# Hybrid block on one Trainium2 core: the two experts picked early run once with 128 places

## Chip, cores and metric

The kernel runs on one core of a Trainium2 chip. The metric is device time in microseconds (us), the median of the timed runs. Three runs of the kernel before took 1964.92, 1969.21 and 1973.45 us.

## What is computed

One layer: a mixer (short convolution and gated DeltaNet), its output projection with a residual, then a mixture of experts with a residual, then a final norm. The change lies in the mixture of experts:

```python
gate, expert_id = ...          # for each of 2048 tokens: one of 4 groups, then the best 2 of its 8 experts
def expert_block(args):        # blocks of tokens of one expert, D = 1024, FF = 512
    xblk, e = args
    return (silu(xblk @ w_gate[e]) * (xblk @ w_up[e])) @ w_down[e]
out = jnp.zeros((N + 1, D)).at[slot_tok].add(yb * slot_gate[:, None])
return rms_norm(x + out, final_norm_g)
```

## The kernel before, in words

All matrices are split into a high and a low float16 half, so each product is three matmuls. The kernel runs in three stages: the mixers; the output projection with the router; the experts.

**Output projection and router.** A loop over 16 tiles of 128 tokens. `tile_a` (L970 to L994) multiplies by `w_out`, adds the residual and writes the normed tile to `h2_d` in DRAM. `tile_b` (L1003 to L1014) turns the tile (8 transposes per half) and makes the 36 router logits. After every 4 tiles (a block of 512 tokens) `route(b)` (L837 to L921) finds, on VectorE, group, experts and each token's place in its expert, and adds them to a table in PSUM (`tabT`, L887).

**The picked experts.** After two blocks `pick` chooses the three experts with the fewest tokens so far (`NSP = 3`), so that their weights are loaded while the projection still runs. Two of them (`NST = 2`) are called job 0 and job 1 here; the third is job 2. Jobs 0 and 1 run in two passes: `first` takes 96 places filled by the first three blocks, fetched in the loop's tile 14; `second` takes 48 places of the last block. `route(2)` and `route(3)` each read the table and write the places (`tabE`, L894; `entries`, L949 to L953), and after `route(2)` a correction (L915 to L920) moves the last block's tokens behind place 96. While `route(3)` and `ranks` (L1193 to L1214, which sorts the other experts by their number of tokens and writes their numbers, `eid`) run on VectorE, TensorE runs the `first` passes: `weave` traces both in turns.

**An expert's work.** `fetch` or `gather` reads the tokens' rows by an indirect DMA of GpSimd (`xr`, L1028) and their gates (L1033); `turn` transposes them (L1044) and copies them to `xT` (L1045); `gate_up` is 192 matmuls (L1059); `down` is 24 matmuls of 512 columns (L1094) if the expert has one chunk of at most 128 places, else 96 matmuls with the operands the other way round (L1129) and transposes back (L1116); ScalarE scales the result by the gate (`yo`, L1103, L1120); GpSimd adds it to `acc_d` in DRAM (L1072).

**Weights.** Each expert has 20 loads on SyncE's queue (L766 twice for each of 8 pieces of gate and up, L775 four times for down): 16 of 256 KB and 4 of 512 KB. They land in staging buffers `mst` (10 of 512 KB at this stage); ScalarE and VectorE (`split`, L92 and L93) make the halves in `wgu` and `wd`, of which there are two each. So job j+2's halves can be made only when `gate_up` of job j is through. The number of the expert is read on SyncE by `value_load` (L1429) from `sid` (the picked ones) or from `eid`.

**Order.** The 32 jobs follow one another; the two outermost of the ranked ones alternate (few and many places), the last three also carry the final norm. A scheduler then places the instructions on the queues by priority; each engine runs its queue in order.

The lines that set it up (before):

```python
C1, C2 = 96, 48
CAPS = [C1 + C2, C1 + C2, 136, 216, 188, 176, 172, 164, ...]
weave((prio(seq(tile_b(NT - 1), route(NB - 1), fetch(second[0]), fetch(second[1]), ranks()),200), 20, 0, 1),
      (seq(gate_up(first[0]), down(first[0]), added(first[0]), gate_up(first[1]), down(first[1]), added(first[1])), 2 * (GU + 6), 0, 1),
      (turn(first[1]), 2, 0.2, 0.4), (prio(turn(second[0]), PT), 2, 0.8, 0.95))
```

## Time and profile before

| | us |
|---|---|
| median of 3 timed runs | 1969.21 |
| span of the profiled execution | 1978.5 |
| TensorE busy | 1774.9 (90%) |
| VectorE busy | 1407.2 (71%) |
| ScalarE busy | 1017.3 (51%) |
| GpSimd busy | 476.2 (24%) |

For the profiled execution only its span, from its first to its last instruction, is given; it is 9.3 us longer than the median of the timed runs. Times in the views are us from the start of that span. The mixers end near 890 us, the projection's last matmul of the loop is at 1146 us, the experts' last matmul at 1907 us, and the rest is the final norm. A busy share is an average over all of these; the change touches the stretch from 1110 us to 1250 us, so that stretch is read by itself.

### The profile page before, as it was taken

The numbers are of one execution on the slowest core, as the hardware profiler recorded it, in microseconds if no ns is written. First come the engines' busy times: TensorE is split into PE (matmuls) and PEld (weight loads), VectorE is DVE, ScalarE is ACT, GpSimd is POOL, SyncE is SP. The second block draws the span as 40 slices with busy tenths as digits, with TensorE's granted clock in tenths as the row PEclk, the third lists the DMA queues.
The fourth block names the chain that finished last, engine by engine and source line by source line (L and its number), as shares of the span: only waits on it lengthen the run. The fifth ranks groups of instructions, "written<-read, shape, count | busy, mean of one in ns | idle before, by whom it ended". The sixth has DMA issues, their size and how long they took to land. (4 is left out here: it accounts for less than half of the span.)

```text
span 1978.5 us, 43091 instructions
## 1 busy us (share of the span) xinstructions
PE 1774.9 (90%) x16783; PEld 1218.3 (62%) x16783; DVE 1407.2 (71%) x2756; ACT 1017.3 (51%) x1700; POOL 476.2 (24%) x408
## 2 busy tenths in 40 slices
PE   6789999999999999999999988998889999999820
PEld 5455555555555554444454466888888999999720
DVE  8889888888888745323246748887778888888623
ACT  6654435345344323211334546776667777767522
POOL 1321211121121100000000114333222443443366
PEclk9889999999999999999999998999999999999965
DMA  4222002002001023002357858999999999999853
GB/s 141 66 67 52 10 15 51 10 16 52 9 13 45 25 66 114 27 17 59 130 173 254 294 169 269 336 312 304 290 308 362 347 334 356 341 342 299 281 162 138
DMA packets 203763, 329.25 MB, mean 166 GB/s; under 512 B 45021, under 2 KB 99366, under 8 KB 203554
## 3 DMA queue, kind: packets, MB, share of 16 engines
q1 hardware_dynamic: 177010, 264.90, 39.9%
q0 software_dynamic: 22016, 52.48, 10.3%
q10 hardware_dynamic: 4528, 9.06, 1.2%
q8 instruction: 133, 2.18, 0.5%
q14 instruction: 76, 0.62, 0.1%
HBM read 276.21 MB, written 54.53 MB: 167 GB/s over the span
## 5 line engine op out<-in xcount | busy, mean ns | idle before, releaser
L134 PE MATMUL acc<-hT,whl 128*128 128x512 f16 x2640 | 635.0, 381 | 0.2 <-DVE hT L203 0.2
L1059 PE MATMUL a<-xT,wgu 128*128 128x136 f16 (+19 forms) x6528 | 407.7, 225 | 22.8 <-DVE sl L1066 13.7
L1059 PEld LDWEIGHTS <-wgu 128*128 128x128 f16 x6528 | 399.3, 100 | 30.4 <-issue 25.9
L134 PEld LDWEIGHTS <-whl 128*128 128x128 f16 x2640 | 253.0, 99 | 248.2 <-issue 11.2
L93 DVE SCALAR_TENSOR_TENSOR wgu<-mst,gw,wgu 128x1024 f16<-128x1024 f32 x256 | 317.2, 1277 | 15.8 <-ACT wgu L92 15.8
L92 ACT ACTIVATE wgu<-mst,gw 128x1024 f16<-128x1024 f32 x256 | 279.0, 1138 | 31.3 <-DMA mst<-in_w_up_dram 28.2
L979 PE MATMUL a<-wo,yb 128*128 128x512 f16 x768 | 178.0, 384 | 0.0
L1072 POOL DMA_INDIRECT acc_d<-yo,tabS x53 | 106.0, 1999 | 257.1 <-ACT yo L1120 200.3
L93 DVE SCALAR_TENSOR_TENSOR wd<-mst,wd 128x1024 f16<-128x1024 f32 x128 | 154.5, 1215 | 6.2 <-ACT wd L92 6.2
L1129 PE MATMUL a<-ac,wd 128*128 128x136 f16 (+12 forms) x1920 | 142.8, 230 | 2.7 <-issue 1.2
L92 ACT ACTIVATE wd<-mst 128x1024 f16<-128x1024 f32 x128 | 130.7, 1045 | 19.4 <-DMA mst<-in_w_down_dram 17.3
L1129 PEld LDWEIGHTS <-wd 128*128 128x128 f16 x1920 | 130.2, 98 | 5.7 <-issue 3.9
L979 PEld LDWEIGHTS <-yb 128*128 128x128 f16 x768 | 72.5, 99 | 80.5 <-issue 5.4
L294 DVE SCALAR_TENSOR_TENSOR cv<-raw,pcol,cv 128x512 f32<-128x512 f32 x144 | 114.9, 800 | 1.6
L1028 POOL DMA_INDIRECT xr<-h_d,tabG x54 | 69.5, 1286 | 171.7 <-PE t L1044 161.8
L1066 DVE SCALAR_TENSOR_TENSOR sl<-a,sl 128x136 f32<-128x136 f32 (+19 forms) x136 | 39.6, 293 | 91.4 <-ACT sl L1065 80.5
L1065 ACT ACTIVATE sl<-a 128x136 f32<-128x136 f32 (+19 forms) x136 | 37.1, 275 | 123.9 <-PE a L1059 101.4
L1094 PE MATMUL pl<-wd,ac 128*120 128x512 f16 (+6 forms) x336 | 80.4, 384 | 0.7 <-ACT ac L92 0.7
L382 DVE TENSOR_TENSOR pr<-Ts,fs 32x1 f32<-32x1 f32 (+14 forms) x240 | 76.6, 319 | 4.0 <-DMA fs<-dscr 0.3
L1116 PE MATMUL pl<-id,yt 128*128 128x128 f32 (+13 forms) x320 | 55.4, 293 | 25.4 <-ACT yo L1120 19.5
L1033 POOL DMA_INDIRECT gs<-gt_d,gix x54 | 74.0, 1371 | 16.4 <-issue 16.0
L545 ACT ACTIVATE osq<-acv 128x512 f32<-128x512 f32 x16 | 10.1, 628 | 125.5 <-DVE acv L543 125.5
(351 smaller groups left out, 2592.3 us busy)
## 6 DMA issues: line engine op xcount, KB each, us to landing
mst<-in_w_gate_dram SPq DMA_DIRECT2D x256, 256.0 KB
mst<-in_w_up_dram SPq DMA_DIRECT2D x256, 256.0 KB
mst<-in_w_down_dram SPq DMA_DIRECT2D x128, 512.0 KB
wst<-in_w_in_dram SPq DMA_DIRECT2D x28, 512.0 KB
xt<-in_x_dram SPq DMA_DIRECT2D x16, 512.0 KB
ydr<-yh SPq DMA_DIRECT2D x64, 128.0 KB
x<-in_x_dram SPq DMA_DIRECT2D x16, 512.0 KB
yb<-ydr SPq DMA_DIRECT2D x16, 512.0 KB
```

The source lines that it names most:

```text
L92: A.activation(hi, src, AF.Copy, scale=scale)
L93: (eng or V).scalar_tensor_tensor(lo, src, scale, hi, op0=OP.mult, op1=OP.subtract)
L134: T.matmul(acc, w[:, i, k, :], hT[b][:, j, k, :], start=(n == 0), stop=(n == 3 * KT - 1))
L294: V.scalar_tensor_tensor(y, tap(j), pcol[:, q:q + 1], y, op0=OP.mult, op1=OP.add)
L382: V.tensor_tensor(q, Ts[:, 0:i, 0:i].rearrange("p j m -> p m j"), bc(fs[:, None, 0:i, i], [32, i, i]), op=OP.mult)
L979: T.matmul(po, yb[:, i, k, c * P:(c + 1) * P], wo[:, j, k, n * FF:(n + 1) * FF], start=(q == 0), stop=(q == 3 * KT - 1))
L1028: G.indirect_dma_start(out=xr[0:cw].rearrange("p a k c -> p (a k c)"), out_offset=None, in_=h2_d[0:end, :], in_offset=IO(ap=ix, axis=0))
L1033: G.indirect_dma_start(out=g[0:cw], out_offset=None, in_=gt_d[0:end * NE, :], in_offset=IO(ap=gx, axis=0))
L1059: T.matmul(pg[:, q, 0:n], wq[:, i, k, q, f * P:(f + 1) * P], xT[:, j, k, 0:n], start=(z == 0), stop=(z == 3 * KT - 1))
L1072: st = G.indirect_dma_start(out=acc_d, out_offset=IO(ap=sx, axis=0), in_=yo[0:cw], in_offset=None, bounds_check=S - 1, oob_is_err=False, c ...
L1094: T.matmul(py[0:n], ac[:, i, k, 0:n], wd[:, j, k, q * FF:(q + 1) * FF], start=(z == 0), stop=(z == 3 * FF // P - 1))
L1129: T.matmul(pg[:, u, 0:n], wd[:, i, k, d * P:(d + 1) * P], ac[:, j, k, 0:n], start=(z == 0), stop=(z == 3 * FF // P - 1))
```

## The change

`first` and `second` become one job each, `early`, of 128 places (`C1 = P`), traced when all four blocks are routed. The table is read once for them, the correction after the third block goes, and so do the two passes over `gate_up` and `down`. The third picked expert has 128 places in place of 136, so one chunk in place of two. The last tile's logits, the rest of `route(2)`, `route(3)`, the fetches, the turn of job 0 and `ranks` are traced one after the other with nothing woven in. And each `value_load` of an expert's number is placed behind the weight load that was traced last (`tc.issue_after`), an order on SyncE's queue and no wait for the load to end. The core of the diff (comments, which were also dropped, are left out):

```diff
-    NST = 2                         # of them in two passes: the first blocks' tokens, the last block's
-    C1, C2 = 96, 48
-    NE1 = S - TB                    # tokens of the first blocks
+    NST = 2
+    C1 = P
-    CAPS = [C1 + C2, C1 + C2, 136, 216, 188, 176, 172, 164, 160, 156, 152, 148, 148, 144, 144, 144, 140, 136, 136, 136,
+    CAPS = [C1, C1, C1, 216, 188, 176, 172, 164, 160, 156, 152, 148, 148, 144, 144, 144, 140, 136, 136, 136,
...
-                nc.sync.dma_start(st, v[:, k, :])
+                lastw[0] = nc.sync.dma_start(st, v[:, k, :]).ins
...
-        if b >= NB - 2:
-            # the first experts' tokens: places below C1, C2 places from there on
-            i = b - (NB - 2)
-            w = (C1, C2)[i]
+        if b == NB - 1:
             V.tensor_copy(tabE, tabT)
             p0 = psL.tile([P, NST], F32, name="pl")
-            T.matmul(p0[0:w], tabE[:, i * C1:i * C1 + w], selT, start=True, stop=True)
-            entries(w, slice(0, NST), i, p0[0:w], (NE1, S)[i], sidf[0:w, 0:NST])
+            T.matmul(p0, tabE[:, 0:C1], selT, start=True, stop=True)
+            entries(C1, slice(0, NST), 0, p0, S, sidf[:, 0:NST])
...
-        if b == NB - 2:
-            # the last block's tokens of the first experts stand behind the first C1 places
-            pc = psL.tile([P, NE], F32, name="pl")
-            T.matmul(pc, on16, Ms[:, (NB - 1) * CB], start=True, stop=True)
...
-        if t == NT - 2:
-            parts.append((seq(rts, gather(first[0], mst, "mst", NE1), gather(first[1], mst, "mst", NE1)),
-                          4, 0, 0.6))
...
-    second = [Job(e, [(tabG[0:C2, e, 1:2], gix[0:C2, e, 1:2], tabS[0:C2, e, 1:2], C2)]) for e in range(NST)]
+    early = [Job(e, [(tabG[0:C1, e, 0:1], gix[0:C1, e, 0:1], tabS[0:C1, e, 0:1], C1)]) for e in range(NST)]
-    jobs = list(second)
+    jobs = list(early)
...
-            eids[r] = nc.sync.value_load(src[0:1, r:r + 1], min_val=0, max_val=NE - 1)
+            with tc.issue_after(lastw[0]):
+                eids[r] = nc.sync.value_load(src[0:1, r:r + 1], min_val=0, max_val=NE - 1)
...
-    drain(turn(first[0]))
-    weave((prio(seq(tile_b(NT - 1), route(NB - 1), fetch(second[0]), fetch(second[1]), ranks()),200), 20, 0, 1),
-          (seq(gate_up(first[0]), down(first[0]), added(first[0]), gate_up(first[1]), down(first[1]), added(first[1])), 2 * (GU + 6), 0, 1),
-          (turn(first[1]), 2, 0.2, 0.4), (prio(turn(second[0]), PT), 2, 0.8, 0.95))
+    drain(prio(seq(tile_b(NT - 1), rts, route(NB - 1), fetch(early[0]), fetch(early[1]), turn(early[0]), ranks()), 200))
```

TensorE has 1116 rows fewer in the changed program. Between the last logits matmul and the first `gate_up` matmul of job 0 its queue then holds 22 matmuls of routing and ranks and 16 transposes, and no expert's matmul. How the queues of the other engines move:

**VectorE, the end of `route(3)`** (`pos`: places of the tokens; `Aoh`, `tabE`: the table; `sl`, `ac`: an expert's `gate_up`; `tabG`, `gix`: row and gate numbers for the fetch). Before:

```order
L876 TENSOR_TENSOR pq<-OH,pl 128x256
L908 TENSOR_TENSOR gt<-gt 128x128
L877 TENSOR_REDUCE pos<-pq 128x2x4
L1066 SCALAR_TENSOR_TENSOR sl<-a,sl 128x96
L884 TENSOR_TENSOR Aoh<-iot,pos 128x864 x2
L93 SCALAR_TENSOR_TENSOR ac<-sl,ac 128x96
L894 CAST tabE<-tabT 32x216
L950 TENSOR_SCALAR tabS<-pl 48x2
```

In the change:

```order
L875 TENSOR_TENSOR pq<-OH,pl 128x256
L876 TENSOR_REDUCE pos<-pq 128x2x4
L883 TENSOR_TENSOR Aoh<-iot,pos 128x864 x2
L891 CAST tabE<-tabT 32x216
L936 TENSOR_SCALAR tabS<-pl 128x2
L1176 COPY key<-pl 128x32
L937 TENSOR_SCALAR gfx<-pl 128x2
```

The `first` passes' steps are gone from between the routing steps; a step of `ranks` stands between those of `entries`.

**SyncE's queue, from job 2's `w_down` loads to the first load of job 3** (`eid`: numbers of the ranked experts; `nblk`: number of overflow blocks; `gfin`: gain of the final norm). Before:

```order
L775 DMA mst<-in_w_down_dram 128x1024
L1429 TENSOR_LOAD eid
L1429 ISA x2
...
L775 ISA
L775 DMA mst<-in_w_down_dram 128x1024
...
L1429 TENSOR_LOAD eid
L1429 ISA x2
L766 ISA
L766 DMA mst<-in_w_gate_dram 128x512
```

In the change:

```order
L775 DMA mst<-in_w_down_dram 128x1024
L1449 DMA gfin<-in_final_norm_g_dram 128x1024
L1472 TENSOR_LOAD nblk
L1472 ISA x2
L775 ISA
L775 DMA mst<-in_w_down_dram 128x1024
...
L1412 TENSOR_LOAD eid
L1412 ISA x2
L766 ISA
L766 DMA mst<-in_w_gate_dram 128x512
```

Before, 11 reads of `eid` stand ahead of job 2's last two loads and 6 more ahead of job 3's first; in the change one stands ahead of each job's loads, and the loads of `gfin` and `nblk` have moved up here.

**GpSimd, from the last block's gates to the first sum** (`xr`: an expert's rows; `gs`: their gates; `acc_d`: the sums). Before:

```order
L909 DMA gt_d<-gt 128x4x32
L1028 DMA xr<-h_d,tabG 48x2048
L1033 DMA gs<-gt_d,gix 48x1
L1028 DMA xr<-h_d,tabG 48x2048
L1033 DMA gs<-gt_d,gix 48x1
L1072 DMA acc_d<-yo,tabS 2048x1024 x2
L1028 DMA xr<-h_d,tabG 128x2048
L1028 DMA xr<-h_d,tabG 8x2048
```

In the change:

```order
L906 DMA gt_d<-gt 128x4x32
L1014 DMA xr<-h_d,tabG 128x2048 x2
L1019 DMA gs<-gt_d,gix 128x1 x3
L1014 DMA xr<-h_d,tabG 128x2048
L1019 DMA gs<-gt_d,gix 120x1
```

The sums of the `first` passes no longer stand between the fetches. From job 4 on the order of TensorE, VectorE and ScalarE is the same in both programs.

## Rows read from the trace of the kernel before

**Rows 1.** The page: the span, TensorE's busy time, and the group of the 192-matmul step.
```profile
span 1978.5 us, 43091 instructions
PE 1774.9 (90%) x16783; PEld 1218.3 (62%) x16783; DVE 1407.2 (71%) x2756; ACT 1017.3 (51%) x1700; POOL 476.2 (24%) x408
L1059 PE MATMUL a<-xT,wgu 128*128 128x136 f16 (+19 forms) x6528 | 407.7, 225 | 22.8 <-DVE sl L1066 13.7
```

**Rows 2.** Windows: PE, PEld, DVE, ACT, POOL busy, PE clock, DMA share, GB/s.
```profile
1200.00:1220.00 20.00, 13.18 (x230) 9.41 (x229) 12.01 (x18) 10.36 (x18) 12.10 (x9) 0.74 0.88 296
1520.00:1540.00 20.00, 19.28 (x298) 18.64 (x296) 18.54 (x25) 16.13 (x24) 6.88 (x4) 1.00 1.05 382
1500.00:1800.00 300.00, 294.77 (x4470) 278.37 (x4468) 262.69 (x380) 227.86 (x330) 121.62 (x79) 1.00 1.02 346
```

**Rows 3.** TensorE's timeline: start, us, line, operation, count; idle before it and its releaser.
```profile
1171.65 0.27 PE L1044 MATMUL t<-id,xr 48*128 48x48 f16 x4 [1.17 <-DMA xr<-h_d,tabG]
1175.43 10.04 PE L1059 MATMUL a<-xT,wgu 128*128 128x96 f16 x208
1195.15 5.36 PE L1094 MATMUL pl<-wd,ac 128*48 128x512 f16 x24
1204.67 0.22 PE L1059 MATMUL a<-xT,wgu 128*128 128x48 f16 x2 [0.51 <-issue]
1213.35 1.57 PE L1059 MATMUL a<-xT,wgu 128*128 128x48 f16 x35 [0.52 <-issue]
1214.74 1.88 PE L1044 MATMUL t<-id,xr 128*128 128x128 f16 x16
1216.55 1.82 PE L1094 MATMUL pl<-wd,ac 128*48 128x512 f16 x4
1224.13 11.35 PE L1059 MATMUL a<-xT,wgu 128*128 128x136 f16 x189
1245.58 9.93 PE L1059 MATMUL a<-xT,wgu 128*128 128x120 f16 x186
```

**Rows 4.** VectorE's timeline, from the last logits to the last block's places.
```profile
1153.96 0.20 DVE L1014 SCALAR_TENSOR_TENSOR L<-pl,lt 128x36 f32<-128x36 f32 x1 [0.29 <-ACT lt L1011]
1156.92 0.55 DVE L1045 COPY xT<-t 128x768 f16<-128x768 f16 x1
...
1165.57 0.37 DVE L894 CAST tabE<-tabT 32x216 f16<-32x216 f32 x1 [0.91 <-PE tabT L887]
```

**Rows 5.** GpSimd's and ScalarE's timelines: a 48-row fetch; a 128-row one and its reader.
```profile
1168.11 0.93 POOL L1028 DMA_INDIRECT xr<-h_d,tabG  x1 [4.90 <-DVE key L1197]
1948.49 1.04 POOL L1368 DMA_INDIRECT mst<-acc_d,bix  x1 [0.30 <-issue]
1953.52 1.06 ACT L1344 ACTIVATE jk<-mst 128x1024 f16<-128x1024 f32 x1 [2.52 <-DMA mst<-acc_d,bix]
```

**Rows 6.** TensorE after a wait near the end: its timeline, and windows around it.
```profile
1896.34 4.63 PE L1059 MATMUL a<-xT,wgu 128*128 128x112 f16 x48 [11.46 <-DVE sl L1066]
...
1896.00:1901.00 5.00, 4.66 (x49) 4.60 (x49) 2.69 (x9) 1.04 (x4) 4.47 (x4) 0.52 0.37 150
1901.00:1905.00 4.00, 3.35 (x16) 1.83 (x15) 1.75 (x3) 0.56 (x2) 3.47 (x4) 1.00 0.64 207
```

**Rows 7.** SyncE's queue: job 2's four w_down loads, then job 3's first load.
```profile
1156.81 36.95 SPq L775 DMA_DIRECT2D mst<-in_w_down_dram  x4
...
1197.45 0.31 SPq L766 DMA_DIRECT2D mst<-in_w_gate_dram  x1
```

**Rows 8.** ScalarE's timeline: job 2's first split, job 3's, and one that waits for its load.
```profile
1188.86 1.15 ACT L92 ACTIVATE wgu<-mst,gw 128x1024 f16<-128x1024 f32 x1 [0.35 <-PE a L1059]
1215.12 1.14 ACT L92 ACTIVATE wgu<-mst,gw 128x1024 f16<-128x1024 f32 x1
1272.50 1.06 ACT L92 ACTIVATE wd<-mst 128x1024 f16<-128x1024 f32 x1 [1.07 <-DMA mst<-in_w_down_dram]
```

**Rows 9.** TensorE's timeline: a wait in the experts' stage.
```profile
1387.93 1.19 PE L1116 MATMUL pl<-id,yt 128*128 128x128 f32 x4 [6.06 <-ACT yo L1120]
```

More of the change, by code (lines that the diff above doesn't have):

```diff
@@ L746, in hybrid_block @@
     W = {}
+    lastw = [None]
     nstage = [0]
@@ L765, in load_part @@
                 for q in range(2):
-                    nc.sync.dma_start(st[:, q], vs[q][:, k, :])
+                    lastw[0] = nc.sync.dma_start(st[:, q], vs[q][:, k, :]).ins
                 split(w[:, 0, k], w[:, 1, k], st, gw[:, k:k + 1])
@@ L820, in hybrid_block @@
     selT = rt.tile([NE, NST], F16, name="selT")
-    ssum = rt.tile([1, NE], F32, name="ssum")
     sbig = rt.tile([P, NE], F32, name="sbig")
@@ L887, in route @@
                 T.matmul(tabT, oht[:, k, c], Aoh[:, c], start=(b == 0 and k == 0 and c == 0),
-                         stop=(b >= NB - 2 and k == 1 and c == CB - 1), skip_group_check=True)
+                         stop=(b == NB - 1 and k == 1 and c == CB - 1), skip_group_check=True)
             yield 1
-        if b >= NB - 2:
-            i = b - (NB - 2)
-            w = (C1, C2)[i]
+        if b == NB - 1:
             V.tensor_copy(tabE, tabT)
             p0 = psL.tile([P, NST], F32, name="pl")
-            T.matmul(p0[0:w], tabE[:, i * C1:i * C1 + w], selT, start=True, stop=True)
-            entries(w, slice(0, NST), i, p0[0:w], (NE1, S)[i], sidf[0:w, 0:NST])
+            T.matmul(p0, tabE[:, 0:C1], selT, start=True, stop=True)
+            entries(C1, slice(0, NST), 0, p0, S, sidf[:, 0:NST])
             yield 1
@@ L911, in route @@
         yield 1
-        if b == NB - 2:
-            pc = psL.tile([P, NE], F32, name="pl")
-            T.matmul(pc, on16, Ms[:, (NB - 1) * CB], start=True, stop=True)
-            cor = o2.tile([1, NE], F32, name="cor")
-            V.tensor_scalar(cor, pc[0:1], float(C1), None, op0=OP.min)
-            V.tensor_scalar(cor, cor, -1.0, float(C1), op0=OP.mult, op1=OP.add)
-            V.tensor_tensor(cor, cor, ssum, op=OP.mult)
-            V.tensor_tensor(Ms[0:1, (NB - 1) * CB], Ms[0:1, (NB - 1) * CB], cor, op=OP.add)
         yield 1
@@ L940, in pick @@
                 V.tensor_scalar(sbig, sel, 1e6, None, op0=OP.mult)
-            if e == NST - 1:
-                V.tensor_scalar(ssum, sbig[0:1], 1.0, None, op0=OP.is_gt)
             yield 1
@@ L1149, in hybrid_block @@
     hid = load_picked()
-    first = [Job(e, [(tabG[0:C1, e, 0:1], gix[0:C1, e, 0:1], tabS[0:C1, e, 0:1], C1)]) for e in range(NST)]
     rts = None
```

## The prediction

> **What bounds the kernel now.** I read the page first, then windows over the stretches of the experts, then each engine's timeline from 1110 to 1280 us. The page shows TensorE busy for 1774.9 of 1978.5 us, the only engine near the span [rows 1]. The windows show that this holds for the experts' stage in full: from 1500 to 1800 us PE is busy for 294.77 of 300 us at a granted clock of 1.00, while the 16 DMA engines have a share of 1.02 and move 346 GB/s [rows 2]. So two things are nearly full there, and whatever comes earlier must come earlier in both. The stretch that the change rewrites looks different: from 1200 to 1220 us PE is busy for 13.18 of 20 us and the clock is 0.74 [rows 2]. TensorE's timeline says what that is: in the 48-place pass of job 1, from 1204.67 to 1213.35 us, 2 and 35 matmuls show pauses ended by "issue" [rows 3], nothing that the profile can name. The jobs form a rigid train behind it: job 3's halves go into the buffers that job 1 frees, at 1214.7 us, and ScalarE's first split for job 3 starts at 1215.12 [rows 8]. The time is therefore set by when job 3 is through on TensorE, and by whether its weights, and those of the jobs behind it, can follow.
>
> **The change part by part.** I follow the chain from the last logits (1153.96 us [rows 4]) to the end of job 3's `gate_up`, which before is 1245.58 + 9.93 = 1255.5 us [rows 3].
>
> *Fetch.* The first fetch of the last block's tokens is issued at 1168.11 us [rows 5]. VectorE's routing chain ahead of it loses what the order shows gone: two copies to `xT` of 0.55 us [rows 4], some small steps of the `first` passes, and waits for TensorE like the 0.91 us ahead of `tabE` [rows 4], of which I count two, since TensorE now has no expert's matmul queued. That is up to 2.9 us. Against that the table's matmuls run behind pauses, at the lower clock: 0.5 us, an estimate. Issue: 1165.7. The landing of 128 rows instead of 48 is not in the early rows; 48 rows took 1168.11 to 1171.65, 3.5 us [rows 3, 5], and a later fetch of 128 rows 1948.49 to 1953.52, 5.0 us [rows 5]. I take 5.0, being the same shape, and keep 3.5 as the other end: 1170.7. Sixteen transposes take 1.88 us [rows 3], and the copy to `xT` 0.7 (0.55 us for 768 columns [rows 4], scaled to 1024): job 0's `gate_up` starts at 1173.3.
>
> *TensorE's clock.* Between 1157 and 1173 us TensorE now has hardly any work: this is a cost that the change adds. The nearest row is the long wait near the end: after 11.46 us without work, 48 matmuls of 112 columns take 4.63 us, 96 ns each; the granted clock is 0.52 in these 5 us and 1.00 in the next 4 [rows 6]. So I let 4.5 us pass at the lower level, 96 ns × 128/112 = 110 ns a matmul, which gives 41 matmuls. One of 128 columns at the upper level I put at 56.7 ns, the mean of 120 columns (9.93 us / 186 = 53.4) and 136 columns (11.35 / 189 = 60.1) [rows 3]. The other 151 take 8.6 us: job 0's `gate_up` ends at 1186.4. The Trainium skill ("TensorE: Matmul & The Clock Gate", "Why this matters for your kernels") advises against idle gaps between bursts of matmuls, as the clock falls back to half; that speaks against this change. If job 0's whole `gate_up` ran at 110 ns, it would cost 21.1 us in place of 13.1, and the result would be 8 us later. Rows 6 agree with the fall, and show the return during the burst, not behind it.
>
> *Jobs 0 to 2.* The 1.88 us for 16 transposes [rows 3] fell at the lower clock, so behind the burst I take about half of it, 1.0. Eight of job 1's, which stand there, 0.5; `down` of job 0 5.4 (24 matmuls of 512 columns, 5.36 [rows 3]), `gate_up` of job 1 192 × 56.7 ns = 10.9: ends 1203.2, against 1214.7 before, so job 3's splits may begin 11.5 us earlier. Job 2's transposes 1.0, its `gate_up` 10.9, `down` of job 1 5.4: 1220.5. `down` of job 2, one chunk now, 5.4, job 3's transposes 0.9: 1226.8. Job 3's `gate_up`, 192 × 53.4 ns = 10.3: 1237.1. TensorE is **18 us ahead** of the program before (1255.5).
>
> *Weights.* SyncE's queue is held from 1156.81 for 36.95 us, to 1193.8, by the last loads of job 2, which wait for staging buffers, and the first load of job 3 goes out at 1197.45, after six reads of `eid` [rows 7]. The buffers come free by job 2's splits, which started at 1188.86 when `gate_up` of job 0 was through [rows 8]; now that is 2.4 us earlier. With one read of the six (each some 0.6 us: 3.7 us for six) the first load goes out at about 1192, **5.4 us ahead**. TensorE's lead of 18 is worth only as much as the loads can follow. In the stretch from 1200 to 1220 they moved 296 GB/s at a share of 0.88, and in one busy window later 382 [rows 2]; 20 us × (382 − 296)/382 gives 4.5 us more; and 52 us to the `w_down` split at 1272.50, which had to wait for its load [rows 8] and so has no reserve, at 382 against 346, give 4.9. The loads' lead there is 14.8, and TensorE's is cut to that: **15 us**. The other 3 are given back in waits at jobs 4 and 5. From job 4 on the order of TensorE is the same, so 15 us goes rigidly to the end.
>
> The Trainium skill ("DMA: Bandwidth & Descriptors", "Specifications") puts a core's share of memory bandwidth at about 358 GB/s. By that 346 is 97% of what there is, and the catching up would hardly occur: 1961, which is a rival below. The trace's window of 382 [rows 2] shows it is no hard limit.
>
> *Costed at nothing.* The loads of `gfin` and `nblk` that moved up in SyncE's queue and the one read of `eid` a job: SyncE waits there for staging buffers to 1193.8 anyway [rows 7]. If `ranks` came after that, each microsecond would delay all weights; but by the order it follows the fetches, and by the chain above it should end some 10 us before the buffers come free. The steps of `route(2)` and the early fetches that go from the loop: TensorE is the loop's bound and they are VectorE's and GpSimd's; a gain of 1 us at most.
>
> **The sum.** 1978.5 − 15 = 1963.5 us of span. The profiled execution stands 9.3 us above the median; I carry that over: 1969.2 − 15 = **1954.0 us**, 0.8% faster. A measurement of this kernel can tell about 0.5% (9.8 us) from no change. Bounds: the landing 3.5 in place of 5.0 (−1.5), the clock's return twice as long (+2.4: 4.5 us at about half the work), VectorE without its 2.9 (+2.9), loads' lead 8 to 18 (+7 to −3): 1947 to 1960.
>
> **Rivals.**
> *B, the transfers hold it.* For it: a share of 1.02 at 346 GB/s in the long stretch, and a split at 1272.50 that waits for its load [rows 2, 8]. Against it: the 382, and the idle share at 1200. Then the lead is the 5.4 of the first load plus (346 − 296)/346 × 20 = 2.9 us: 8 us, **1961**.
>
> *D, the lead also removes later waits.* Further on, TensorE waits 6.06 us at 1387.93 for ScalarE's `yo` [rows 9], which stood behind splits that waited for loads. If the loads run ahead enough, no 3 us is given back and this wait goes: 18 + 6 = 24, **1945**. Against it: the loads must be another 9 us ahead by then, with no buffers to hold them.
>
> *C, slower: the clock stays down.* If TensorE remains at the lower level through jobs 0 and 1, `gate_up` costs 192 × (110 − 56.7) = 10.2 us more for each, and `down`, at 455 ns a matmul (4 in 1.82 us at the lower clock) in place of 223 [rows 3], 5.6 more. Less the 2.2 already counted for job 0: 29 us, so that 18 ahead become 11 behind: **1980**. Each microsecond at the lower level costs 0.48; it decides from 18/0.48 = 37 us more at that level for no gain at all. For it: short bursts with pauses kept the clock at 0.74 from 1200 to 1220 [rows 2]. Against it: the return within 5 us [rows 6], and 24 long matmuls behind each `gate_up`.
>
> *E, the change doesn't do what it says: an expert has more than 128 tokens.* Then an overflow block runs at the end, a job's 192 + 24 matmuls with loads that nothing hides: some 60 us, an estimate. The inputs give the picked three 85, 104 and 103 tokens, and `gate_up` had 6528 = 34 × 192 matmuls before [rows 1], so no block ran. It would be 2030.
>
> **How the numbers follow.** My forecast A has 0.62, B 0.20, D 0.11, C 0.06, E 0.01. Faster by over 0.5% (below 1959.4) are A, but for 0.01, and D: 0.72. Within 0.5%: that 0.01 and most of B, 0.19: 0.20. Slower: C, E and 0.01 of a B in which the fetch too is late: 0.08. The range takes A (1947 to 1960), B with 6 us lost on the way up to 1967, and part of D to 1943: 1943 to 1967.
>
> **What would show it.** TensorE's timeline: job 0's `gate_up` starts near 1173, its first 4.5 us at the lower clock, ends near 1186; the "issue" pauses of the 48-place pass are gone; job 3's `gate_up` ends near 1237. SyncE's queue: job 3's first load near 1192. Waits ended by DMA or `yo` near 1260 to 1290 that add some 3 us. If job 3 is 18 us ahead and the end only 8, B is right; if the granted clock reads 0.5 beyond 1185, C.

## The result, and the profile after

| | before | changed |
|---|---|---|
| median of 5 timed runs, us | 1969.21 (1964.92 to 1973.45) | 1956.44 (1952.52 to 1960.18) |
| ratio | | 0.9927, 95% interval 0.9906 to 0.9948 |
| span of the profiled execution, us | 1978.5 | 1954.7 |

The change is faster by 12.8 us by the medians and by 14.4 us (10 to 19) by the ratio; 15 were forecast. In a later group of runs (e5) the ratio was 0.9938 (0.9921 to 0.9955). The two profiles stand 23.8 us apart, more than the times: one profiled execution is one draw, and chips differ (the kernel before took 1970 us on the chip of one group below and 1978 to 1979 us on those of two others). So times are compared within a group only. Stretches are counted **from the end of the loop's last `w_out` matmul**, 1145.7 us in the profile of before and 1141.7 us after; the 4.0 us between these two are not all the change's.

The page of the changed kernel shows 384 `gate_up` matmuls fewer, two times 192 [rows 1], and 25.7 us less work for TensorE:

```profile
span 1954.7 us, 41851 instructions
PE 1749.2 (89%) x16213; PEld 1197.7 (61%) x16213; DVE 1403.5 (72%) x2720; ACT 1007.6 (52%) x1674; POOL 457.3 (23%) x398
L1045 PE MATMUL a<-xT,wgu 128*128 128x128 f16 (+17 forms) x6144 | 394.1, 227 | 16.6 <-DVE sl L1052 15.7
```

VectorE's, GpSimd's and SyncE's timelines, in this order: the last logits, the table, the 128-row fetch, job 2's last two `w_down` loads, and job 3's first load. They answer to [rows 4, 5, 7].

```profile
1150.22 0.20 DVE L1000 SCALAR_TENSOR_TENSOR L<-pl,lt 128x36 f32<-128x36 f32 x1 [3.32 <-ACT lt L997]
1160.68 0.37 DVE L891 CAST tabE<-tabT 32x216 f16<-32x216 f32 x1 [0.97 <-PE tabT L886]
...
1162.91 1.07 POOL L1014 DMA_INDIRECT xr<-h_d,tabG  x1 [5.42 <-DVE ohr L1186]
...
1184.74 1.73 SPq L775 DMA_DIRECT2D mst<-in_w_down_dram  x2
1188.62 0.34 SPq L766 DMA_DIRECT2D mst<-in_w_gate_dram  x1
```

TensorE's timeline, job 0's transposes to job 4's (rows of jobs 0 to 4; it answers to [rows 3]):

```profile
1167.27 1.89 PE L1030 MATMUL t<-id,xr 128*128 128x128 f16 x16 [2.96 <-DMA xr<-h_d,tabG]
1169.84 0.48 PE L1045 MATMUL a<-xT,wgu 128*128 128x128 f16 x3 [0.68 <-DVE xT L1031]
...
1170.96 11.02 PE L1045 MATMUL a<-xT,wgu 128*128 128x128 f16 x189
...
1187.79 10.88 PE L1045 MATMUL a<-xT,wgu 128*128 128x128 f16 x192
...
1221.74 10.36 PE L1045 MATMUL a<-xT,wgu 128*128 128x120 f16 x192
...
1238.44 0.74 PE L1030 MATMUL t<-id,xr 88*128 88x88 f16 x8 [5.02 <-DVE xT L1031]
```

The 5.02 us are the largest wait of TensorE in this stretch, and new: before, the same transposes waited 1.06 us. What they wait for is seen on ScalarE and VectorE, whose queues are in order: a split of job 4's `w_down` waits for its load, job 3's `ac` stands behind it, and the copy to `xT` behind that:

```profile
1234.52 1.06 ACT L92 ACTIVATE wd<-mst 128x1024 f16<-128x1024 f32 x1 [1.31 <-DMA mst<-in_w_down_dram]
1235.49 0.29 ACT L92 ACTIVATE ac<-sl 128x120 f16<-128x120 f32 x1
...
1235.80 0.28 DVE L93 SCALAR_TENSOR_TENSOR ac<-sl,ac 128x120 f16<-128x120 f32 x1 [1.14 <-ACT ac L92]
...
1237.72 1.28 DVE L1031 COPY xT<-t 128x1024 f16<-128x1024 f16 x2
```

Windows (columns as in rows 2): the pause before job 0, its `gate_up`, and the stretch in which the loads catch up.

```profile
1160.00:1167.00 7.00, 1.50 (x11) 0.73 (x9) 5.40 (x31) 0.00 (x0) 3.35 (x3) 0.50 0.29 86
1167.00:1172.00 5.00, 4.05 (x41) 3.89 (x42) 3.05 (x10) 0.00 (x0) 3.85 (x4) 0.54 0.71 212
1172.00:1177.00 5.00, 5.00 (x93) 5.00 (x91) 2.90 (x16) 0.59 (x2) 1.95 (x2) 1.00 0.28 91
...
1196.00:1216.00 20.00, 19.76 (x286) 16.67 (x284) 20.00 (x28) 15.93 (x25) 5.60 (x3) 1.00 1.04 376
1216.00:1260.00 44.00, 38.98 (x436) 32.77 (x434) 35.56 (x44) 31.16 (x42) 10.45 (x7) 0.92 1.04 341
```

The table counts us from the end of the loop; "forecast" is the prediction's figure less 1145.7, and for job 4 the 135.2 of before less the lead of 14.8. The second and third profile of before are e1 and e9 below, the second after is e5.

| | before, three profiles | changed, two | forecast |
|---|---|---|---|
| the loop's last tile takes | 15.3, 15.6, 15.8 | 13.7, 13.4 | |
| job 0's `gate_up` starts | | 28.2, 28.2 | 27.6 |
| job 0's `gate_up` ends | | 40.3, 40.5 | 40.7 |
| job 1's `gate_up` ends | 69.2 (first profile) | 57.0, 57.2 | 57.5 |
| job 3's first load | 51.7, 51.6, 51.4 | 46.9, 47.2 | 46.3 |
| job 3's `gate_up` ends | 109.8, 109.6, 109.2 | 90.4, 90.7 | 91.4 |
| job 4's `gate_up` ends | 135.2, 135.0, 134.6 | 122.4, 123.1 | 120.4 |
| job 8's `gate_up` ends | 226.1, 226.3, 228.4 | 214.8, 214.8 | |
| job 13's `gate_up` ends | 354.6, 350.9, 354.6 | 336.3, 336.2 | |

TensorE's lead is 19 us at job 3, 12 at job 4, 11 to 14 at job 8. With the 2 us of the loop's last tiles this gives some 14, which is near what the times show; how far such a sum holds is said under "Costed at nothing".

### The profile page after: what moved, and what is told of

The parts are those of the page before. It is cut to its first block, busy times and chain, and to the rows that moved or that the text cites. A ratio compares the mean times of both kernels' runs of the same rounds, so it can differ in the third digit from the quotient of the medians.

```text
span 1954.7 us, 41851 instructions
## 1 busy us (share of the span) xinstructions
PE 1749.2 (89%) x16213; PEld 1197.7 (61%) x16213; DVE 1403.5 (72%) x2720; ACT 1007.6 (52%) x1674; POOL 457.3 (23%) x398
## 5 line engine op out<-in xcount | busy, mean ns | idle before, releaser
L1045 PE MATMUL a<-xT,wgu 128*128 128x128 f16 (+17 forms) x6144 | 394.1, 227 | 16.6 <-DVE sl L1052 15.7
L1045 PEld LDWEIGHTS <-wgu 128*128 128x128 f16 x6144 | 388.7, 99 | 22.8 <-issue 16.8
L92 ACT ACTIVATE wgu<-mst,gw 128x1024 f16<-128x1024 f32 x256 | 280.3, 1139 | 30.7 <-DMA mst<-in_w_up_dram 29.1
L1058 POOL DMA_INDIRECT acc_d<-yo,tabS x50 | 95.8, 1915 | 251.5 <-ACT yo L1106 189.4
L1115 PE MATMUL a<-ac,wd 128*128 128x144 f16 (+12 forms) x1824 | 136.3, 230 | 1.3 <-ACT ac L92 1.2
L1115 PEld LDWEIGHTS <-wd 128*128 128x128 f16 x1824 | 124.2, 98 | 4.0 <-issue 2.3
L1014 POOL DMA_INDIRECT xr<-h_d,tabG x51 | 59.4, 1165 | 171.0 <-PE t L1030 165.0
L1052 DVE SCALAR_TENSOR_TENSOR sl<-a,sl 128x128 f32<-128x128 f32 (+17 forms) x128 | 38.2, 300 | 75.5 <-ACT sl L1051 75.0
L1051 ACT ACTIVATE sl<-a 128x128 f32<-128x128 f32 (+17 forms) x128 | 35.7, 280 | 108.7 <-PE a L1045 105.9
L1019 POOL DMA_INDIRECT gs<-gt_d,gix x51 | 76.7, 1504 | 15.6 <-issue 15.3
L1080 PE MATMUL pl<-wd,ac 128*128 128x512 f16 (+4 forms) x312 | 75.3, 388 | 1.0 <-ACT ac L92 0.8
```

Of the source, the lines that this page charges most:

```text
L92: A.activation(hi, src, AF.Copy, scale=scale)
L1014: G.indirect_dma_start(out=xr[0:cw].rearrange("p a k c -> p (a k c)"), out_offset=None, in_=h2_d[0:end, :], in_offset=IO(ap=ix, axis=0))
L1019: G.indirect_dma_start(out=g[0:cw], out_offset=None, in_=gt_d[0:end * NE, :], in_offset=IO(ap=gx, axis=0))
L1045: T.matmul(pg[:, q, 0:n], wq[:, i, k, q, f * P:(f + 1) * P], xT[:, j, k, 0:n], start=(z == 0), stop=(z == 3 * KT - 1))
L1058: st = G.indirect_dma_start(out=acc_d, out_offset=IO(ap=sx, axis=0), in_=yo[0:cw], in_offset=None, bounds_check=S - 1, oob_is_err=False, c ...
L1080: T.matmul(py[0:n], ac[:, i, k, 0:n], wd[:, j, k, q * FF:(q + 1) * FF], start=(z == 0), stop=(z == 3 * FF // P - 1))
```

## The experiments

**e1 and e9: the kernel before, unchanged.**

> The kernel before, unchanged: how far two executions of one program differ. Theory: the profiled execution of before (span 1978.5 us) was a slow draw, since its median was 1969.2; a second one has a span of 1963 to 1972, and the 10 us less are in the waits of 4 to 6 us of TensorE for ScalarE's yo in jobs 9 to 13, which depend on when loads land, and a few us in the mixers. Rival: the span of 1978.5 is what the profiler makes of this program always; then the second one is again within 3 us of it and the 23.8 us between the two profiles are the change's. Ratio expected 0.998 to 1.002.

Ratio 0.9995 (0.9984 to 1.0007); the span was 1972.1 us on a chip on which before takes 1979.2. TensorE's waits at jobs 9, 11 and 13 were 3.98, 4.56 and 3.49 us (the second ended by a split on VectorE, the others by `yo`) where the first profile had 6.06 [rows 9], 4.60 and 3.99, all for `yo`. So a profile of one program moves by some us, and the 23.8 us between the two profiles are not the change's alone. The theory's 1963 to 1972 was just missed, and its reason (a slow draw) is not the whole of it: chips differ too.

> The kernel before, unchanged, beside three others on one chip. Theory: the pauses that the profile ends by issue (9 us of them in the 48-place pass and the transposes ahead of it) belong to the passes, so they are here again, with 7 to 10 us, and the end of job 3's gate_up comes 109 to 110 us after the loop. Rival: they belong to the chip of the first profile (its time of 1978.5 is that of the chip of the second group, 1979, not that of 1969); then on a chip with 1969 they are under 3 us, and job 3 ends 103 to 106 us after the loop.

Ratio 0.9998 (0.9988 to 1.0008), span 1984.6. The pauses are here again, in all profiles of before. The waits of TensorE (waited for, total us, times, longest), first profile and this one:

```profile
PE a L1059 <- issue: 6.8, 11, 1.2
PE t L1044 <- issue: 2.4, 5, 0.5
```

```profile
PE a L1059 <- issue: 6.4, 12, 1.1
PE t L1044 <- issue: 2.7, 3, 1.2
```

The changed kernel has no such row in that stretch. The theory's figures are met, but the rival is not tested by this: the chip is again one of the slower kind (1978), and a profile of before on a chip with 1970 is missing. The first profile looks like one of the slower kind too: in every other run the profiled execution took 1.7 to 1.9 us more than its span, so that of 1978.5 took some 1980 us, more than any of its five timed runs (to 1973.45). And the runs below speak for the rival: in job 0's `gate_up` the relatives of the changed kernel on the slower chips (e3, e4, e11, e12) have such pauses, those on the chip with 1970 (e5 to e8) have none. How much of the gain on a chip with 1970 comes from the pauses stays open.

**e2 and e3: the reads of `eid`.** e2 puts them behind the loads in the kernel before; e3 takes that out of the changed one:

```diff
-            with tc.issue_after(lastw[0]):
-                eids[r] = nc.sync.value_load(src[0:1, r:r + 1], min_val=0, max_val=NE - 1)
+            eids[r] = nc.sync.value_load(src[0:1, r:r + 1], min_val=0, max_val=NE - 1)
```

> Before, with only the reads of eid placed behind the latest weight load (two passes and the third expert stay). Theory: SyncE reads while it would wait anyway; job 3's first load goes out some 3 us earlier (six reads of 0.6 us less one), but job 3's splits still begin when job 1's gate_up ends, so the time is that of before within 4 us (1965 to 1973). Rival: the queue of the loads sets the time, and the reads are what the change gains by: 1957 to 1962.

> The changed kernel, with the reads of eid left where the scheduler puts them by itself. Theory: job 3's first load goes out about 3 us later than in the changed kernel's trace (1188.6 becomes about 1192), the loads' lead falls by as much, and the time rises by 0 to 4 us: 1956 to 1961. Rival: the reads are needed, for without them the loads are as late as before: 1964 to 1970.

e2: 0.9991 (0.9978 to 1.0004), and job 3's first load 51.7 us after the loop, as before: not even the load goes out earlier. e3: 0.9902 (0.9887 to 0.9917), 1961.2 us against 1979.2. Its first load of job 3 comes 6.6 us after job 0's `gate_up`, exactly as in the changed kernel (51.4 − 44.8, and 46.9 − 40.3). Both rivals fall, and so does what both theories said of the load, that the reads move it by 3 us. No run shows a worth of the reads; as the changed kernel itself did not run on e3's chip, a few us either way are not excluded there.

e3 showed something else: job 0's `gate_up` took 16.3 us in place of 12.1. TensorE's timeline of e3, and its windows behind it:

```profile
1172.34 0.48 PE L1045 MATMUL a<-xT,wgu 128*128 128x128 f16 x3 [0.92 <-issue]
...
1178.08 10.56 PE L1045 MATMUL a<-xT,wgu 128*128 128x128 f16 x159 [1.04 <-issue]
```

```profile
1169.00:1174.00 5.00, 3.55 (x33) 3.39 (x34) 2.36 (x7) 0.00 (x0) 3.78 (x5) 0.50 0.43 118
1174.00:1179.00 5.00, 3.95 (x37) 3.61 (x36) 0.89 (x4) 0.00 (x0) 2.08 (x3) 0.50 0.24 88
1179.00:1184.00 5.00, 5.00 (x72) 5.00 (x71) 2.75 (x15) 0.65 (x3) 0.00 (x0) 0.77 0.00 0
```

Two pauses of 1 us by "issue", and the granted clock stays at 0.50, the lower level, until 1179; in the first profile after it was 1.00 from 1172 on. e4, e11 and e12, on the chips with 1978 to 1979, show 14.2 to 14.4 us for the same step; e5, e7 and e8, on that with 1970, show 12.2 to 12.3. In those three it is not the clock: it is back as early as in the changed kernel, and most of what is added are pauses ended by "issue", 1.4 to 1.8 us within the step. TensorE's timeline of e4, and a window:

```profile
1169.20 0.27 PE L1045 MATMUL a<-xT,wgu 128*128 128x128 f16 x2 [0.29 <-issue]
1170.63 8.54 PE L1045 MATMUL a<-xT,wgu 128*128 128x128 f16 x150 [1.16 <-issue]
```

```profile
1167.00:1172.00 5.00, 3.55 (x58) 3.33 (x57) 2.57 (x16) 0.00 (x0) 1.98 (x2) 0.97 0.24 87
```

**e4: the third expert in two chunks again.**

```diff
-    CAPS = [C1, C1, C1, 216, 188, 176, 172, 164, 160, 156, 152, 148, 148, 144, 144, 144, 140, 136, 136, 136,
+    CAPS = [C1, C1, 136, 216, 188, 176, 172, 164, 160, 156, 152, 148, 148, 144, 144, 144, 140, 136, 136, 136,
```

> The changed kernel with 136 places in two chunks for the third picked expert, as before. From the traces the stretch from the end of its gate_up to job 3's takes about 4 us more in that form, and its gate_up 0.5. Theory: TensorE is 23 us ahead at job 3 and only 17 at job 4, where the loads hold it, so 4.5 us less at job 3 are not seen at job 4: the time stays within 3 us of the changed kernel (1954 to 1960). Rival: each microsecond of TensorE counts, 1961.

0.9927 (0.9914 to 0.9940). From job 0's `gate_up` to the end of job 3's it takes 58.4 us (101.1 − 42.7) against 50.1 (90.4 − 40.3): 8 us more, twice what was expected. At job 4's end 83.1 against 82.1 remain of it: 1 us. Against e3, on the same chip and counted from the loop, it is 5.4 us at job 3 (101.1 and 95.7) and 1.5 at job 4 (125.8 and 124.3). So TensorE's lead at job 3 is cut at job 4, as the theory says. By time it is 0.25% behind e3 on the same chip, 5 us, with intervals that barely overlap; so one chunk may be worth something that the theory doesn't see.

**e5: the changed kernel again.**

> The changed kernel, unchanged, beside the others of this group: ratio to before expected 0.989 to 0.994 (0.9927 at first). Theory: what differs from run to run after the change is how soon TensorE's clock comes back in job 0's gate_up; counted from the loop's last w_out matmul that gate_up ends after 40 us (first profile) or up to 45 (as in the two kernels near it), and the end of job 4's gate_up comes after 122 to 126 us. Rival: that 45 belongs to the kernels with late reads or the wide third expert; then this one is at 40 again.

0.9938 (0.9921 to 0.9955), 1959.2 against 1970.4 us. Job 0's `gate_up` ends at 40.5, so the range up to 45 is not this program's on this chip.

**e6: TensorE kept busy through the routing.** New lines, with `fill(14)` behind the logits and 7, 6 and 18 more behind three routing steps:

```diff
+    def fill(n, after=None):
+        p = psA.tile([P, 2, 256], F32, name="a")
+        q = wr.rearrange("p k h c -> p (k h c)")[:, 0:512]
+        for i in range(n):
+            with tc.issue_after(lastm[0] if after is None else after):
+                lastm[0] = T.matmul(p.rearrange("p a b -> p (a b)"), on16, q, start=True, stop=True).ins
```

> The changed kernel with 45 matmuls of 512 columns of constants, whose result nobody reads, in TensorE's pauses between the last logits and job 0's transposes (14 behind the logits, 7 behind the places, 6 behind the table, 18 behind the ranks). It computes the same. Theory: the low clock costs the changed kernel 1.3 to 6 us in job 0's gate_up (12.2 us in the first profile, 16 in a second, against 10.9 at the upper clock) and 2 us in routing and transposes; with the filler gate_up of job 0 ends 37 to 38 us after the loop instead of 40 to 45, the loads of job 3 go out as much earlier, and the time falls by 2 to 6 us against the changed kernel. Rival 1, the loads hold everything from job 4 on whatever TensorE does: within 1 us. Rival 2, the filler stands in the way of routing's matmuls: slower by 1 to 3 us.

0.9946 (0.9925 to 0.9966), beside e5's 0.9938: nothing gained. TensorE's timeline of e6, and a window:

```profile
1170.02 10.88 PE L1059 MATMUL a<-xT,wgu 128*128 128x128 f16 x192
```

```profile
1167.00:1172.00 5.00, 4.49 (x63) 3.68 (x61) 4.12 (x20) 0.00 (x0) 1.32 (x2) 1.00 0.43 162
```

The clock is kept (1.00 where it was 0.54) and `gate_up` takes the 10.9 us of a warm one. But seven matmuls of filler stand between the transposes, and it starts 29.1 us after the loop instead of 28.2: it ends 0.3 us earlier (0.5 against e5), and of that at most 0.4 is left at job 4 (122.7; changed 122.4, e5 123.1). The step is 1.2 us shorter than in the changed kernel, but there eight of job 1's transposes stand inside it (0.85 us, from 1170.11 to 1170.96) and here behind it. The low clock's price for the 192 matmuls is thus some 0.4 us (0.6 in e5). Rival 1 fits: the medians (1957.6 and e5's 1959.2) and the ratios point opposite ways, both within the noise. Of rival 2 the later start is seen, but no loss of time.

**e7: eleven staging buffers.**

```diff
-    mst2 = moe.enter_context(tc.tile_pool(name="mst2", bufs=5, side="right", reuse_waits="tile"))
-    stages[:] = [mst, mst2]
+    mst2 = moe.enter_context(tc.tile_pool(name="mst2", bufs=6, side="right", reuse_waits="tile"))
+    stages[:] = [mst, mst2] * 5 + [mst2]
```

> The changed kernel with eleven staging buffers of 512 KB instead of ten from job 3 on (some of the router's buffers single instead of double). It computes the same. Theory (the loads hold the lead at jobs 4 to 13): one load more can be under way, which is 1.5 us at 346 GB/s, while SyncE waits for job 2's splits; job 3's first load goes out 1 to 2 us earlier, and the time falls by 1 to 4 us against the changed kernel. Rival (TensorE holds it): within 1 us.

0.9938 (0.9923 to 0.9953), as e5. Job 3's first load goes out at 44.8 instead of 47.2, earlier even than expected, and job 4 ends at 123.0, as in e5. So it is not when job 3's first load goes out that decides; e8 tests how fast the loads go.

**e8: fewer bytes.**

```diff
+                if isinstance(key, int) and key >= NSP:
+                    lastw[0] = nc.sync.dma_start(st[:, 0:512], v[:, k, 0:512]).ins
+                    sb = bc(st[:, None, 0:512], [P, 2, 512])
+                    split(w[:, 0, k].rearrange("p (a b) -> p a b", a=2), w[:, 1, k].rearrange("p (a b) -> p a b", a=2), sb, WS)
```

> The changed kernel in which the experts from job 3 on load only the first 512 columns of w_down and use them twice: it leaves out half of w_down's bytes (1 MB of 6 for each job), with the same number of splits and matmuls. Theory (transfers cut the lead from 19 us at job 3 to 13 at job 4 and cause the waits of 2 to 5 us for yo in jobs 7 to 13, 13.6 us in all): job 4 keeps 17 to 19 us, the waits shrink to under 4 us in all, and the time falls by 10 to 18 us against the changed kernel. Rival (TensorE, with ScalarE's and VectorE's splits in its way, holds the stage, and the loads only fill what room there is): the time falls by 0 to 4 us.

0.9871 (0.9853 to 0.9889), 15.2 us below e5 by the medians and 13 by the ratios. TensorE's timeline of e8, the wait at job 4, one for `yo`, and two windows:

```profile
1232.98 0.47 PE L1035 MATMUL t<-id,xr 88*128 88x88 f16 x8 [1.74 <-DVE xT L1036]
...
1364.50 1.20 PE L1107 MATMUL pl<-id,yt 128*128 128x128 f32 x4 [4.20 <-ACT yo L1111]
```

```profile
1216.00:1260.00 44.00, 42.13 (x485) 36.70 (x484) 35.90 (x48) 31.33 (x45) 10.54 (x7) 0.96 1.02 331
...
1500.00:1800.00 300.00, 294.96 (x4560) 281.36 (x4558) 260.90 (x382) 225.79 (x331) 125.86 (x80) 1.00 0.95 294
```

The wait at job 4 falls from 5.64 (e5) to 1.74, and job 4 ends at 118.9 instead of 123.1: the loads' rate is what cuts the lead. Of the 10.5 us that e8 is ahead of e5 at job 31 by the traces, 4.2 come here and 7.2 between jobs 28 and 30, where e5's wait of 4.93 us for `yo` is gone. But in jobs 7 to 13 the waits for `yo` stay (2.10, 4.20, 2.44 and 2.88 us; e5: 2.18, 5.10, 3.17 and 1.88). There the theory falls: bytes are not their cause, or not alone, and what is stays open. From 1500 to 1800 us TensorE is just as busy with 294 GB/s as with 346 [rows 2], so the transfers do not hold that stretch.

**e10: the second passes with 96 places.**

```diff
-    C1, C2 = 96, 48
+    C1, C2 = 96, 96
```

> The kernel before with 96 places instead of 48 in the second passes (the additional places are empty; it computes the same). At the upper clock the pass of job 0 should take 4 to 5 us more than with 48. Theory: matmuls of 48 columns, 27 ns each, run out of instructions, so the 48-place pass of job 1 takes 14.3 us for what could be 5.2; with 96 columns at 48 ns it takes 9 to 11 us without pauses, and the two passes together are within 2 us of before: same time within 3 us. Rival: the pauses come from the loads that start just then (from 1197 us on), whatever the width; then the pass of job 1 takes 15 to 19 us, and the time is 5 to 9 us above before.

1.0022 (1.0010 to 1.0033), 4 us slower. TensorE's timeline of e10, the pass of job 1 and what follows, and a window:

```profile
1201.92 8.32 PE L1059 MATMUL a<-xT,wgu 128*128 128x96 f16 x192
1216.41 1.89 PE L1044 MATMUL t<-id,xr 128*128 128x128 f16 x16 [6.17 <-issue]
```

```profile
1211.00:1216.00 5.00, 0.00 (x0) 0.00 (x0) 0.00 (x0) 4.95 (x6) 3.78 (x5) 0.93 1.05 386
```

Neither expectation was met. The pass runs without a pause in 8.32 us, and then TensorE stands still for 6.17 us, again ended by "issue": 14.5 us together, where 48 columns took 14.3. So these 14.3 us hold for either number of columns, and halving the columns bought nothing in this pass; in job 0's it bought 2.5 us (6.8 from start to end with 48, 9.3 with 96). The time, 4 us slower, comes near the rival's 5 to 9, but its longer pass did not occur. That the loads run at full rate just then (1.05, 386 GB/s) is not enough for a cause, as the changed kernel has 1.04 and 376 GB/s with TensorE busy for 19.76 of 20 us. What the engine lacks there was not tested further.

**e11: six us of useless work ahead of job 3.**

```diff
+        if j == 3:
+            drain(fill(27))
         weave(*parts)
```

> The changed kernel with 27 matmuls of 512 columns (6.0 us at the upper clock) of constants ahead of job 3's gate_up on TensorE; it computes the same. Theory (the give-back of the prediction: at job 4 TensorE waits 5.0 to 5.6 us for copies that stand behind w_down splits that wait for loads): job 3's gate_up ends 6 us later, 96 to 97 us after the loop, the wait at job 4 shrinks to under 1 us, job 4 ends 0 to 2 us later, and the time rises by 0 to 2 us. Rival (every microsecond of TensorE's lead goes to the end): 6 us.

0.9912 (0.9896 to 0.9928), beside 0.9916 for e12 on the same chip. TensorE's timeline of e11:

```profile
1222.74 5.99 PE L990 MATMUL a<-wr,on 128*128 128x512 f16 x27
...
1238.49 2.68 PE L1056 MATMUL a<-xT,wgu 128*128 128x120 f16 x48 [2.20 <-DVE sl L1063]
```

Counted from the end of job 0's `gate_up` (42.6), job 3 ends after 58.2 us (changed: 50.1), and job 4 after 82.9 (82.1). Eight us later at job 3 are 0.8 at job 4. Job 3's end is later than the 96 to 97 us expected (100.8 from the loop): job 0's `gate_up` ends 2.3 us later on this chip, and the 2.20 us above are a new wait within the step. The wait at job 4 is gone, as expected. The changed kernel itself did not run on this chip, so the time is only held against e12; the trace shows the theory's give-back.

**e12: the splits of job 4's `w_down` later.**

```diff
+                with (tc.issue_after(lastac[0]) if key == K4[0] else ExitStack()):
+                    split(w[:, 0, k], w[:, 1, k], st, WS)
```

Here `lastac` is the last split of job 3's `gate_up`, and job 4's `w_down` is traced behind its transposes.

> The changed kernel in which the four splits of job 4's w_down stand behind job 3's last step of gate_up on ScalarE and VectorE, instead of between them; it computes the same. Theory: the wait of 5 us ahead of job 4 comes from these splits, which stand in the queue ahead of the steps that TensorE needs and wait for their loads, and not from weights that TensorE needs (the halves of job 4's gate and up are ready 15 us ahead); so it shrinks to under 2 us, job 4's gate_up ends 3 to 5 us earlier (118 to 120 us after the loop), and the time falls by 2 to 5 us against the changed kernel. Rival (the loads themselves hold it): the wait comes back within the next jobs, job 8 ends at 214 to 215 us again, time within 1 us.

0.9916 (0.9899 to 0.9932). TensorE's timeline of e12:

```profile
1238.24 3.45 PE L1082 MATMUL pl<-wd,ac 128*120 128x512 f16 x15 [2.26 <-ACT ac L92]
...
1264.80 0.94 PE L1117 MATMUL a<-ac,wd 128*128 128x216 f16 x3 [2.63 <-ACT ac L92]
```

The wait for `xT` is gone, and job 4 ends 77.9 us after job 0's `gate_up` instead of 82.1, as expected. But 2.26 us come back at once, 2.63 at job 4's `down`, and job 5 ends after 107.6 us against 104.9 in the changed kernel. The rival holds in the trace: the order of the queues chooses where the wait falls, the loads decide that it falls. That any version beats the changed kernel is not shown, e8 with its fewer bytes apart: the ratios of e3, e11 and e12 are lower, but from chips on which the changed kernel itself did not run.

## Why the prediction was right

The forecast of 1954.0 lay 2.4 us below the measured 1956.4, with the way through the program as forecast, and with two terms whose errors cancel. The forecast span, 1963.5, lay 8.8 above the measured 1954.7: the 9.3 us carried over from before were no fixed distance between span and time (it is 1.7 us here) but a slower execution. The time does not suffer from it, as the 15 us were taken off the median.

**What bounds.** Right up to job 4: TensorE and the transfers together, with job 3 as the point where the rest hangs on. Not for the long stretch, which the prediction called nearly full in both: from 1500 to 1800 us e8 moves 294 GB/s in place of 346 with TensorE no busier, so the transfers do not hold it.

**The fetch.** Up to 2.9 us less on VectorE were counted; from the logits to `tabE` it went from 11.6 to 10.5 us, 1.15. The 128 rows landed in 4.4 us (1162.91 to 1167.27) where 5.0 were taken and 3.5 to 5.0 bounded. The start of job 0's `gate_up` came 0.6 us later than forecast.

**TensorE's clock.** 4.5 us of `gate_up` at the lower level were counted. In both profiles of the changed kernel itself the clock came back during the transposes and the first matmuls (0.54 from 1167 to 1172, 1.00 from 1172), and `gate_up` took 12.1 us instead of 13.1, eight of job 1's transposes included, which the prediction counted apart. On slower chips its like took 14 to 16 us, most often by pauses at the upper level (e4, e11, e12). Only in e3 did the clock stay at 0.50 longer, until 1179: rival C's mechanism exists, some 3 us of it and not 29. The Trainium skill ("TensorE: Matmul & The Clock Gate", "Why this matters for your kernels") warns of idle gaps between bursts. The trace agrees that the clock falls; e6 shows that here avoiding it is worth nothing that can be measured.

**Jobs 0 to 2.** Right to 1 us by these profiles: job 3 ends 19 us ahead, 18 forecast, because the passes went, and the pauses with them (TensorE's work is 25.7 us less in all). That the passes are the main part follows from e2 (the reads alone gain nothing) and e4 (without the third expert's smaller size the ratio is still 0.9927). With both profiles from one chip the lead is 14 us (109.6 in e1, 95.7 in e3) and 16 (109.2 in e9, 93.4 in e12), so part of the 19 may be the chip's.

**The weights: the term that was mis-sized.** The loads' lead was added up to 14.8 us at the `w_down` split that started at 1272.50 before. That split is job 5's, and its like starts 12.3 us ahead (126.8 and 114.5 from the loop's end). By parts: job 3's first load went out 4.5 to 4.8 us ahead, 5.4 forecast; job 4's first load 11.0 ahead (74.5 and 63.5), so 6.2 were gained where 4.5 were counted; and from there to the split 1.3, where 4.9 were counted by running at 382 against 346. The 382 did not last: 348 GB/s in the 20 us from the first load on, 376 from 1196 to 1216, but 341 from 1216 to 1260. And the stretch of before to catch up with moved 338, at a full share. ScalarE's timeline of the changed kernel, job 5's split, and that window of before:

```profile
1256.19 1.06 ACT L92 ACTIVATE wd<-mst 128x1024 f16<-128x1024 f32 x1
```

```profile
1220.00:1272.00 52.00, 49.93 (x689) 44.85 (x688) 46.59 (x71) 39.94 (x56) 20.18 (x12) 1.00 1.04 338
```

The figure in GB/s counts all transfers. By queue (packets, MB, share of the engines' time; q1 carries the loads, q0 GpSimd's fetches and sums) the window with 382, 1520 to 1540 before, held almost nothing but loads; from 1216 to 1260 in the changed kernel q0 takes 21.9% of the time:

```profile
q1 hardware_dynamic: 3488, 7.39, 100.0%
q0 software_dynamic: 71, 0.21, 4.3%
...
q1 hardware_dynamic: 5755, 12.57, 81.7%
q0 software_dynamic: 811, 2.33, 21.9%
```

So the loads moved 370 GB/s in the first and 286 in the second. That q0's work is the reason was not tested.

TensorE was cut to 12 to 13 us of lead instead of 14.8, and gave back 6 to 7 us and not 3. The wait of 5.0 to 5.6 us at job 4 (1.06 before) is most of that. The rest is a price that the prediction did not count: behind the wait the granted clock is down. TensorE's timeline of the changed kernel and of e11, where that wait is gone, and a window of the changed kernel:

```profile
1240.02 6.32 PE L1080 MATMUL pl<-wd,ac 128*120 128x512 f16 x21
...
1243.41 4.71 PE L1091 MATMUL pl<-wd,ac 128*120 128x512 f16 x21
```

```profile
1238.00:1243.00 5.00, 4.55 (x24) 2.89 (x24) 4.41 (x7) 1.84 (x3) 0.99 (x1) 0.50 1.05 238
```

e4 and e11 (8 us of TensorE vanish at job 4), e7 (an earlier first load changes nothing) and e8 (fewer bytes give 4.2 us) show that this cut is the transfers'. It was rival B's mechanism, working near the size that A had: B's 8 us held 2.9 of gain between the first load and the next stretch, where 6.2 were measured. Of the rule on a core's share of bandwidth ("DMA: Bandwidth & Descriptors", "Specifications", in the Trainium skill) the trace says: 376 and 386 GB/s are seen over 20 and 5 us, 331 to 346 over longer stretches with a full share.

**Costed at nothing.** The reads showed no worth (e2, e3). The steps that left the loop were put at 1 us at most; the loop's last tile is 1.9 us shorter (means of the table), and the one before it 0.3 (12.24 to 11.97): 2.2. This is the second mis-sized term, and it makes up for most of the first: 12.2 at job 4 + 2.2 = 14.4 against 15. That two errors cancel is luck, and that the sum closes so well is luck too. With both profiles from one chip (e1 and e3) the lead is 10.7 at job 4 (135.0 and 124.3) and 7.1 at TensorE's last matmul (757.7 and 750.6), while the times there differ by 18 us; those two profiled executions differ by 6.7 us only (1973.9 and 1967.2). One profile a kernel cannot close a sum to less than several us.

**The rivals.** D failed: the waits for `yo` at jobs 9, 11 and 13 stayed (4.39, 5.10 and 2.01 us), and not even e8 removed them. E did not occur: 6144 = 32 × 192 matmuls. That job 13 is further ahead by the traces (15 to 18 us) than by the times is not explained; the profiles of before vary by 4 us there, and none is known to come from a chip with 1970.

## What to carry to other kernels

Splitting a step so that its first half can start early costs a second pass, and that pass may not be shorter for having fewer columns; price it by its time in the trace, here 14.3 us for job 1's 48 columns, in profiles that come, or seem to come, from the slower chips, against 10.9 for 128 in one pass. When work on the bounding engine goes, follow the lead from job to job to the first point where another stream (here the weights) has no reserve: what is beyond that stream's lead is given back there, whatever made it. And take the rate at which the stream can catch up from a stretch as long as the one it must cover, with the same other transfers in it, not from its best window.

## What was not expected of the hardware

TensorE can stand for 6 us with nothing that the profile names, with 192 matmuls just done (e10), or take the same time in eleven pauses of half a us to 1.2 us between short ones (before). Whether its instructions came late was not tested, and is a rival to every reading of these pauses. The page lists a queue q8 that carries instructions (133 packets before, 129 after, where 570 matmuls are fewer). Around the long pauses 16 to 17 us pass between two of its packets (1189.47 and 1205.60 before, 1190.41 and 1207.83 in e10), in the changed kernel at most 12.1 from 1168 to 1235. But e10's pause begins behind the second packet, and the short pauses of before near 1172 have no such gap, so a late packet alone does not explain them.

Job 0's `gate_up` took 12.1 to 12.3 us in the first profile after and on the chip with 1970, and 14.2 to 16.3 on two others, in nearly the same program; the changed kernel itself was not run on those two, so chip and edit are not fully told apart.
